# Turned probabilities copied by ScalarE between the two sides' exponentials, masked ones against differences of values

## The chip, the core and the metric

The kernel runs on one core of a Trainium2 chip. The metric is device microseconds of one execution, the median of several. Five engines run side by side, each through its own queue in order: TensorE (PE in the profile, its weight loads PEld), VectorE (DVE), ScalarE (ACT), GpSimd (POOL) and SyncE (SP), which here only issues transfers. An engine waits for another through semaphores.

## The reference

One layer of a decoder over 1024 prompt tokens and 8 x 4 sample tokens, in float32, D = 1024. The part that the change touches is the attention of the prompt over a sliding window of 128 keys, with 8 heads in 2 key-value groups of 4 and a learned sink for each head:

```python
def _sink_attention(q, k, v, mask, sinks):
    s = jnp.einsum('bnqhgd,bnkhd->bnhgqk', q, k).astype(jnp.float32) * (HEAD_DIM ** -0.5)
    s = jnp.where(mask[None, :, None, None], s, -jnp.inf)
    sink = sinks.astype(jnp.float32)[None, None, :, :, None, None]
    m = jnp.maximum(jnp.max(s, axis=-1, keepdims=True), sink)
    p = jnp.exp(s - m)
    denom = jnp.sum(p, axis=-1, keepdims=True) + jnp.exp(sink - m)
    w = (p / denom).astype(v.dtype)
    return jnp.einsum('bnhgqk,bnkhd->bnqhgd', w, v)
```

Each of the 8 blocks of 128 queries looks at its own block's keys up to the query and at the previous block's keys behind it. Around it stand the input projection (q, k, v and a pooling mixer), the output projection with norms, a SwiGLU feed-forward and a gated per-layer input.

## The kernel before

Matrix products are made of three float32r matmuls for each tile (high x high, high x low, low x high); "splits" (L173 on ScalarE, L174 on VectorE) make the high and low parts of weights and activations. The stages are the input projections (to about 128 us), the attention with the first output projections between its blocks (to about 214 us), the rest of the output projection, the feed-forward, and the gated input.

In the attention each block goes through these steps. A "side" is one key-value group, four heads; a key and the one 128 before it share a column, since a query sees just one of the two.

- `scores(b)`: matmuls on TensorE; four copies from PSUM on ScalarE (L775) and four predicated copies on VectorE (L779), which put the current block's score or the previous block's score into one tile `t` of 128 columns a head. For block 0 VectorE adds a mask instead (L781).
- `weigh(t)`: for each of the two sides a `softmax`: the maximum (L721), its negative with scale and sink (`nmx`, L723) and the sink's part (`es`, L725) on VectorE; on ScalarE the exponential of `es` (L729) and four exponentials of a head each, with sums (L732); the sum and reciprocal on VectorE (L737, L738); the scaling by it on GpSimd (L740).
- `turned(b, t)`: four transposes a side on TensorE into one PSUM bank (L122), then two multiplications by a mask on VectorE, from that bank: `ptc` (L800) keeps what belongs to the current block's values, `ptp` (L802) what belongs to the previous block's. Block 0 has no `ptp`.
- `values(b, parts)`: for each half of the queries a matmul a side on `ptc`, then one on `ptp`, summed in PSUM; `put` brings the result to the operands of the output projection (L711 on ScalarE, L712 on VectorE). The values stand in `vtok` by block and in `vmix` with the two blocks' halves mixed.

The blocks go in the order 6, 7, 5, 0, 1, 2, 3, 4. One turn of the loop does: scores and weights of the next block, a filler, `turned` and, after another filler, `values` of this one. A filler is a piece of the output projection: `out_pool` and `out_attn` with 12 matmuls, `out_proj` with 24. Behind `out_attn`, VectorE adds (L912), and ScalarE squares (L899, L902) and scales (L914); behind `out_proj`, ScalarE scales (L922) and squares (L902). Behind `out_pool` ScalarE copies (L893).

On TensorE the order is the written one. On the other engines a scheduler decides it when the program is built, except for instructions that `keep_in_program_order` pins among themselves. In the attention before, only the last turn's VectorE instructions are pinned (through `fix`). Tiles named `a` come from one pool of 30 slots.

Of the kernel before, what the change touches and what calls it, by code (L numbers as in the profile page):

```python
# [12 lines left out]
AF = mybir.ActivationFunctionType  # L13
ALU = mybir.AluOpType
AX = mybir.AxisListType

P = 128
# [3 lines left out]
NDEC, DSEQ = 8, 4  # L21
# [11 lines left out]
NB = SEQ // WIN  # L33
# [12 lines left out]
NEG = -1.0e30  # L46
# [16 lines left out]
def trunk_kernel(  # L63
# [33 lines left out]
    te, ve, se, ge = nc.tensor, nc.vector, nc.scalar, nc.gpsimd  # L97
# [10 lines left out]
    def nm(s):  # L108
        cnt[0] += 1
        return f"{s}{cnt[0]}"  # L110

    def act_tile(shape, dt=F32, s="a"):
        return apool.tile(shape, dt, tag="a", bufs=A_SLOTS, name=nm(s))
# [6 lines left out]
    def mt(out, src):  # L120

        ins = te.transpose(out, src, ident)  # L122
        if pinned[0]:
            tc.keep_in_program_order(ins)

    def mm(*args, **kw):

        ins = te.matmul(*args, **kw)  # L128
        if pinned[0]:
            tc.keep_in_program_order(ins)  # L130

    def bank():
        return psum.tile([P, 512], F32, tag="b", name=nm("b"))
# [33 lines left out]
    def fix(ins):  # L167

        if fixed[0]:
            tc.keep_in_program_order(ins)  # L170
# [493 lines left out]
    nc.scalar.dma_start(ps_o, pso)  # L664


    misc = act_tile([P, 6, P])
    qd, am, vdec = misc[:, 0, :], misc[:, 1:5, :], misc[: NDEC * DSEQ, 5, :]
    for c in range(4):
        ge.tensor_copy(  # L670
            qd.rearrange("p (g c e) -> p g c e", g=4, c=4)[:, :, c, :],
# [6 lines left out]
    ge.tensor_scalar(nskd, skd, -1.0, None, op0=ALU.mult)  # L678


    vtok, vmix = act_tile([P, NB, P]), act_tile([P, NB, P])

    def v_turned():
        for h in range(2):
            ps = bank()
            for i in range(4):
                b = 4 * h + i
                mt(ps[:, i * P : (i + 1) * P], vT[:, b * P : (b + 1) * P])
            v = ps.rearrange("p (b c) -> p b c", c=P)
            se.copy(vtok[:, 4 * h : 4 * h + 4, :], v)  # L690
            ge.tensor_copy(vmix[0:64, 4 * h : 4 * h + 4, :], vtok[0:64, 4 * h : 4 * h + 4, :])
        ge.tensor_copy(vmix[64:P, 1:NB, :], vtok[64:P, 0 : NB - 1, :])
        ps = bank()
        mt(ps[: NDEC * DSEQ, :P], vT[:, SEQ:])
        se.copy(vdec, ps[: NDEC * DSEQ, :P])
        nc.scalar.dma_start(kp_o, kT[:, SEQ - WIN : SEQ])
        nc.scalar.dma_start(vp_o, vtok[:, NB - 1, :])
# [17 lines left out]
    def softmax(*parts):  # L715

        scale = 0.125
        held = []
        for t, nh, sk, nsk in parts:
            mx = spool.tile([P, nh], F32, tag="mx", name=nm("mx"))  # L720
            fix(ve.tensor_reduce(mx, t, axis=AX.X, op=ALU.max))  # L721
            nmx = spool.tile([P, nh], F32, tag="nmx", name=nm("nmx"))
            fix(ve.scalar_tensor_tensor(nmx, mx, -scale, nsk, op0=ALU.mult, op1=ALU.min))  # L723
            es = spool.tile([P, nh], F32, tag="es", name=nm("es"))
            fix(ve.tensor_tensor(es, sk, nmx, op=ALU.add))  # L725
            held.append((nmx, es))
        sums = []
        for (t, nh, _, _), (nmx, es) in zip(parts, held):
            se.activation(es, es, AF.Exp)  # L729
            sm = spool.tile([P, nh], F32, tag="sm", name=nm("sm"))  # L730
            for c in range(nh):
                se.activation(  # L732
                    t[:, c, :], t[:, c, :], AF.Exp, bias=nmx[:, c : c + 1], scale=scale, accum_out=sm[:, c : c + 1]
                )
            sums.append(sm)
        for (t, nh, _, _), (_, es), sm in zip(parts, held, sums):
            fix(ve.tensor_tensor(sm, sm, es, op=ALU.add))  # L737
            fix(ve.reciprocal(sm, sm))  # L738
            nk = t.shape[2]
            ge.tensor_tensor(t, t, sm.unsqueeze(2).to_broadcast([P, nh, nk]), op=ALU.mult)  # L740

    def m4(i):
        return am[:, i, :].unsqueeze(1).to_broadcast([P, 4, WIN])

    def v4(a):
        return a.rearrange("p (c k) -> p c k", k=WIN)

    def scores(b, now_=True):


        t = act_tile([P, 8, WIN])
        nk = 2 * WIN if b else WIN
        lo = b * WIN + WIN - nk
        at = WIN * 4 // nk
        both = [[bank() for _ in range(4 // at)] for _ in range(2)]
        sides = [(0, 64, 64, 0, 192), (64, P, 64, 128, 128), (64, P, 192, 64, 64)] if b else [(0, P, 0, 0, nk)]
        for c in range(4):
            i = c % at
            for q0, q1, at0, k0, n in sides:
                for kv in range(2):  # L760
                    rows = slice(64 * kv, 64 * kv + 64)
                    mm(
                        both[kv][c // at][q0:q1, i * nk + at0 : i * nk + at0 + n],
                        qT[c][rows, b * WIN + q0 : b * WIN + q1],
                        kT[rows, lo + k0 : lo + k0 + n],
                        start=True,
                        stop=True,
                    )
        for kv in range(2):
            tk = t[:, 4 * kv : 4 * kv + 4, :]  # L770
            for i, ps in enumerate(both[kv]):
                tc_ = tk[:, i * at : (i + 1) * at, :]
                v = ps.rearrange("p (c k) -> p c k", k=nk)
                if b:
                    se.copy(tc_, v[:, :, 64:192])  # L775
                    m = am[:, 0, :].rearrange("p (h k) -> p h k", h=2).unsqueeze(1).to_broadcast([P, at, 2, 64])
                    other = v[:, :, 192:].unsqueeze(2).to_broadcast([P, at, 2, 64])
                    tch = tc_.rearrange("p c (h k) -> p c h k", h=2)
                    ve.copy_predicated(tch, m.bitcast(mybir.dt.int32), other)  # L779
                else:  # L780
                    ve.tensor_tensor(tc_, v, m4(1), op=ALU.add)  # L781
        if now_:
            weigh(t)
        return t

    def weigh(t):
        for kv in range(2):
            hs = slice(4 * kv, 4 * kv + 4)
            softmax((t[:, hs, :], 4, skp[:, hs], nskp[:, hs]))

    def turned(b, t):

        ptc = act_tile([P, 8, WIN])
        ptp = act_tile([P, 8, WIN]) if b else None
        for kv in range(2):
            ps = bank()
            hs = slice(4 * kv, 4 * kv + 4)
            for c in range(4):
                mt(ps[:, c * P : (c + 1) * P], t[:, 4 * kv + c, :])
            fix(ve.tensor_tensor(ptc[:, hs, :], v4(ps), m4(2), op=ALU.mult))  # L800
            if b:
                fix(ve.tensor_tensor(ptp[:, hs, :], v4(ps), m4(3), op=ALU.mult))  # L802
        return ptc, ptp

    def values(b, parts):


        ptc, ptp = parts
        sides = [(kv, slice(64 * kv, 64 * kv + 64), slice(4 * kv, 4 * kv + 4)) for kv in range(2)]
        if not b:  # L810
            o = bank()
            for kv, cols, hs in sides:
                mm(o[cols, :], vtok[:, b, cols], ptc[:, hs, :], start=True, stop=True)
            put(o, 0, WIN)
            return
        q = [slice(0, 64), slice(64, P)]
        os_ = [bank() for _ in range(2)]
        for i, v in enumerate((vmix, vtok)):
            for kv, cols, hs in sides:
                mm(os_[i][cols, :256], v[:, b, cols], ptc[:, hs, q[i]], start=True, stop=False)  # L820
        for i in range(2):
            for kv, cols, hs in sides:
                mm(os_[i][cols, :256], vtok[q[i], b - 1, cols], ptp[q[i], hs, q[i]], start=False, stop=True)
        for i in range(2):
            put(os_[i], b * WIN + 64 * i, 64)

# [117 lines left out]
    t = scores(order[0], False)  # L944
# [1 line left out]
    filler(1)  # L946
    od = bank()
    pt = dturned(td)
    weigh(t)
    filler(2)  # L950
    ahead = scores(order[1])
    dvalues(pt, od)
# [7 lines left out]
    for a, b in zip(order, order[1:] + [None]):  # L960

        fixed[0] = lazy[0] = b is None
        t2 = ahead or (None if b is None else scores(b))
        ahead = None
        filler(1)
        parts = turned(a, t)
        if b is None:
            lazy[0] = False
            weights(WOA[1][0], 1)
        filler(1)  # L970
        values(a, parts)
        t = t2
# [192 lines left out]
    os_ = [None] * G  # L1165
# [309 lines left out]
def _layout(i):  # L1475

    f = lambda a: np.asarray(a, dtype=np.float32) if not isinstance(a, np.ndarray) else a
    i = {k: f(v) for k, v in i.items()}
# [7 lines left out]
    gains = np.stack([i[n][0].reshape(KC, P).T for n in ("norm_mix_pre", "norm_mix_post", "norm_ffn_pre", "norm_ffn_post")], 1)  # L1486
    sinks = i["attn_sinks"][0]
    q, c = np.arange(WIN)[:, None], np.arange(WIN)[None, :]
    masks = np.stack([1.0 * np.where(q < 64, c <= q, c > q), np.where(c <= q, 0.0, NEG), 1.0 * ((q <= c) | ((q >= 64) & (c < 64))), 1.0 * (q > c)], 1)
    r = np.arange(P)[:, None]  # L1490
    ri, rj = (r % 8) // DSEQ, r % DSEQ
    rb = 2 * (r // 32) + ri
# [57 lines left out]
```

## Time and profile before

| what | before |
|---|---|
| median of 3 runs | 1076.01 us |
| the runs | 1075.78, 1076.01, 1079.14 us |
| the profiled execution's own time | 1077.23 us |
| its span, first to last instruction | 1075.4 us |
| granted TensorE clock, mean | 0.999 |
| attention stage, 127 to 215 us: VectorE busy | 70.36 us of 88 |
| the same: ScalarE busy | 63.19 us of 88 |

The profile is of one execution. A row of its groups gives the line, the engine, the operation, output and input tiles without their numbers, the shape, the count, the busy time and the mean length, then the idle time of the engine just ahead of it and who ended it. A row of the timeline gives start, length and the same names, with x the number of merged instructions. Starts follow each other more closely than the lengths, since the instructions of an engine overlap a little.

### The profile page before, as it was taken

Reading aid. Unit: us, or ns where it says so; the run is one execution under the profiler, and the core shown is the slowest. Engines: PE = TensorE matmul, PEld = TensorE weight load, DVE = VectorE, ACT = ScalarE, POOL = GpSimd, SP = SyncE. Lnnn points to the kernel's source line nnn. Section 1 sums busy time; section 2 is a strip of 40 time slices with the busy share of each in tenths; the row PEclk is TensorE's granted clock in tenths of the full one; section 3 lists DMA queues with packets and bytes.
Section 4 is the critical chain, followed back from the end, with each engine's and each line's share of the span. In section 5 each row is a group of like instructions: output and inputs, shape, how many; then the busy total and the mean of one; then the engine's idle time right before and its main releaser. Section 6 shows DMA issues by size and latency. Waiting matters only on the chain.

```text
span 1075.4 us, 18180 instructions
## 1 busy us (share of the span) xinstructions
PE 1068.5 (99%) x7107; PEld 1051.6 (98%) x7107; DVE 872.4 (81%) x1303; ACT 512.2 (48%) x872; POOL 275.6 (26%) x211
## 2 busy tenths in 40 slices
PE   9999999999999999999999999999999999999998
PEld 8999988899999999999999999999999999999998
DVE  6876378886979957796698898898899998969983
ACT  7423277664555533445543443443444465545441
POOL 0073032100000024444444454454442000023300
PEclk9999999999999999999999999999999999999999
DMA  8121311544544422422212213212234556464361
GB/s 300 59 73 40 104 58 37 202 157 144 200 165 137 137 99 79 138 74 84 84 70 86 91 60 98 79 60 98 79 114 174 179 170 249 153 212 156 99 211 62
DMA packets 43574, 130.91 MB, mean 122 GB/s; under 512 B 5060, under 2 KB 15716, under 8 KB 43488
## 3 DMA queue, kind: packets, MB, share of 16 engines
q1 hardware_dynamic: 42160, 127.98, 34.9%
q10 hardware_dynamic: 1328, 1.77, 0.5%
q8 instruction: 56, 0.92, 0.3%
q14 instruction: 30, 0.25, 0.1%
HBM read 113.86 MB, written 15.87 MB: 121 GB/s over the span
## 4 chain that ended last, share of the span: by engine, by line
PE 95%; ACT 2%; DVE 2%; DMA 0%; issue 0%; SPq 0%; ACTq 0%; DVEq 0%
PE b L128 95%; ACT a L732 1%; DMA xr<-in_x_dram 0%; DVE mx L721 0%; PE b L122 0%; DVE a L779 0%; DVE wl L174 0%; DVE ml L712 0%; ACT wh L173 0%; DVE sm L737 0%; DVE a L781 0%; ACT y L914 0%; ACT sq L902 0%; ACT y L922 0%; ACT es L729 0%
## 5 line engine op out<-in xcount | busy, mean ns | idle before, releaser
L1108 POOL TENSOR_TENSOR wr<-wr,wr 128x512 f32<-128x512 f32 x108 | 170.0, 1588 | 480.0 <-DMA wr<-in_w_gu_dram 247.9
L173 ACT CAST wh<-wr 128x1024 fp32r<-128x1024 f32 (+1 forms) x138 | 142.0, 1031 | 165.2 <-PE b L128 97.9
L174 DVE TENSOR_TENSOR wl<-wr,wh 128x1024 fp32r<-128x1024 f32 (+1 forms) x138 | 172.7, 1254 | 42.4 <-ACT wh L173 21.2
L128 PE MATMUL b<-fh,wh 128*128 128x352 f32 x624 | 201.5, 323 | 0.0
L128 PE MATMUL b<-fh,wl 128*128 128x352 f32 x624 | 200.0, 320 | 0.0
L128 PE MATMUL b<-fl,wh 128*128 128x352 f32 x624 | 199.9, 320 | 0.0
L128 PE MATMUL b<-fh,sh 128*128 128x352 f32 x416 | 134.3, 323 | 0.0
L128 PE MATMUL b<-fl,sh 128*128 128x352 f32 x416 | 133.3, 320 | 0.0
L128 PE MATMUL b<-fh,sl 128*128 128x352 f32 x416 | 133.3, 320 | 0.0
L173 ACT CAST sh<-wr 128x1024 fp32r<-128x1024 f32 x72 | 75.7, 1052 | 120.1 <-POOL wr L1108 119.7
L174 DVE TENSOR_TENSOR sl<-wr,sh 128x1024 fp32r<-128x1024 f32 x72 | 98.3, 1366 | 36.1 <-ACT sh L173 20.0
L128 PEld LDWEIGHTS b<-fh,wh 128*128 128x128 f32 x624 | 117.0, 187 | 0.4
L128 PEld LDWEIGHTS b<-fl,wh 128*128 128x128 f32 x624 | 117.2, 188 | 0.0
L128 PEld LDWEIGHTS b<-fh,wl 128*128 128x128 f32 x624 | 117.1, 188 | 0.0
L128 PE MATMUL b<-h,wh 128*128 128x352 f32 x480 | 105.3, 324 | 0.6 <-ACT h L449 0.3
L128 PE MATMUL b<-hid,wh 128*128 128x352 f32 x416 | 99.4, 322 | 0.0
L128 PEld LDWEIGHTS b<-h,wh 128*128 128x128 f32 x480 | 81.6, 188 | 2.1 <-DVE h L451 1.2
L128 PEld LDWEIGHTS b<-fl,sh 128*128 128x128 f32 x416 | 78.2, 188 | 0.0
L128 PEld LDWEIGHTS b<-fh,sh 128*128 128x128 f32 x416 | 78.0, 188 | 0.1
L128 PEld LDWEIGHTS b<-fh,sl 128*128 128x128 f32 x416 | 78.0, 188 | 0.0
L1108 POOL TENSOR_TENSOR wr<-wr 128x512 f32<-128x512 f32 x36 | 50.2, 1393 | 108.1 <-DVE w L174 103.6
L128 PE MATMUL b<-hp,sh 128*128 128x352 f32 x320 | 76.4, 322 | 0.0
(202 smaller groups left out, 2217.9 us busy)
## 6 DMA issues: line engine op xcount, KB each, us to landing
wr<-in_w_gu_dram SPq DMA_DIRECT2D x88, 512.0 KB, 3.3
wr<-in_w_dn_dram SPq DMA_DIRECT2D x40, 512.0 KB, 3.3
wr<-in_w_pg_dram SPq DMA_DIRECT2D x16, 512.0 KB, 3.6
x<-in_x_dram SPq DMA_DIRECT2D x6, 704.0 KB, 8.6
x1d<-x SPq DMA_DIRECT2D x6, 704.0 KB, 3.6
x<-x1d SPq DMA_DIRECT2D x6, 704.0 KB, 5.1
out_y_dram<-yo SPq DMA_DIRECT2D x24, 176.0 KB, 2.1
wr<-in_w_out_b_dram SPq DMA_DIRECT2D x8, 512.0 KB, 3.3
```

The source lines that it names most:

```text
L128: ins = te.matmul(*args, **kw)
L173: fix(se.copy(hi, src))
L174: fix(ve.tensor_tensor(lo, src, hi.bitcast(F32), op=ALU.subtract))
L732: se.activation(t[:, c, :], t[:, c, :], AF.Exp, bias=nmx[:, c : c + 1], scale=scale, accum_out=sm[:, c : c + 1])
L1108: ge.tensor_tensor(out, a, b, op=op)
```

## The change

The probabilities for the current block are no longer masked. ScalarE copies them whole from PSUM into `ptc`. What belongs to the previous block is then counted with the current block's values too, and the masked part `ptp` meets the difference of the two blocks' values (`vdif`, made once by GpSimd), which takes the wrong one out and puts the right one in. For block 0 the probabilities above the diagonal are zero already. The number and shapes of matmuls stay as they were.

The order is changed with it. `scores` now weighs only side 0 of the next block; side 1 is weighed after this block's `turned`. All exponentials of heads and the new copies are pinned in the order written, so that the copies stand between the two sides' exponentials on ScalarE.

```diff
-    vtok, vmix = act_tile([P, NB, P]), act_tile([P, NB, P])
+    vtok, vmix, vdif = (act_tile([P, NB, P]) for _ in range(3))
...
         ge.tensor_copy(vmix[64:P, 1:NB, :], vtok[64:P, 0 : NB - 1, :])
+        ge.tensor_tensor(vdif[:, 1:NB, :], vtok[:, 0 : NB - 1, :], vtok[:, 1:NB, :], op=ALU.subtract)
...
             for c in range(nh):
-                se.activation(
-                    t[:, c, :], t[:, c, :], AF.Exp, bias=nmx[:, c : c + 1], scale=scale, accum_out=sm[:, c : c + 1]
+                tc.keep_in_program_order(
+                    se.activation(
+                        t[:, c, :], t[:, c, :], AF.Exp, bias=nmx[:, c : c + 1], scale=scale, accum_out=sm[:, c : c + 1]
+                    )
                 )
...
         if now_:
-            weigh(t)
+            weigh(t, 0)
         return t
 
-    def weigh(t):
-        for kv in range(2):
+    def weigh(t, *sides):
+        for kv in sides:
...
-            fix(ve.tensor_tensor(ptc[:, hs, :], v4(ps), m4(2), op=ALU.mult))
+            tc.keep_in_program_order(se.copy(ptc[:, hs, :], v4(ps)))
             if b:
-                fix(ve.tensor_tensor(ptp[:, hs, :], v4(ps), m4(3), op=ALU.mult))
+                fix(ve.tensor_tensor(ptp[:, hs, :], v4(ps), m4(2), op=ALU.mult))
...
-                mm(os_[i][cols, :256], vtok[q[i], b - 1, cols], ptp[q[i], hs, q[i]], start=False, stop=True)
+                mm(os_[i][cols, :256], vdif[q[i], b, cols], ptp[q[i], hs, q[i]], start=False, stop=True)
...
-    weigh(t)
+    weigh(t, 0, 1)
...
         parts = turned(a, t)
+        if t2:
+            weigh(t2, 1)
```

The table of masks loses the one that `ptc` met, so that `m4(2)` is now what `m4(3)` was.

The order of instructions shows what the scheduler made of it. First, ScalarE in the turn of block 7, where the scores in `a_1650` (before) or `a_1652` (now) are block 5's. Before:

```order
L173 CAST wh_1980<-wr_1949 128x1024
L732 ACTIVATE a_1650,sm_1694<-a_1650,nmx_1689 128x128 x2
L729 ACTIVATE es_1691<-es_1691 128x4
L732 ACTIVATE a_1650,sm_1694<-a_1650,nmx_1689 128x128 x2
L729 ACTIVATE es_1706<-es_1706 128x4
L732 ACTIVATE a_1650,sm_1709<-a_1650,nmx_1704 128x128 x4
L893 COPY y_1286<-b_1717 128x352
L893 COPY y_1287<-b_1747 128x352
```

The same place now; `a_1718` is `ptc` of block 7:

```order
L173 CAST wh_1982<-wr_1936 128x1024
L730 ACTIVATE es_1693<-es_1693 128x4
L734 ACTIVATE a_1652,sm_1696<-a_1652,nmx_1691 128x128 x4
L896 COPY y_1286<-b_1704 128x352
L803 COPY a_1718<-b_1720 128x512
L803 COPY a_1718<-b_1727 128x512
L730 ACTIVATE es_1738<-es_1738 128x4
L734 ACTIVATE a_1652,sm_1741<-a_1652,nmx_1736 128x128 x4
L896 COPY y_1287<-b_1749 128x352
```

The two copies stand behind one side's exponentials and behind the copy of a filler's result, and ahead of the other side's exponentials.

Second, ScalarE in the turn of block 1; the scores are block 2's (`a_2023`, now `a_2025`). Before:

```order
L173 CAST wh_2124<-wr_1984 128x1024
L711 CAST mh_2019<-b_2016 128x4x128
L775 COPY a_2023<-b_2024 128x256
L775 COPY a_2023<-b_2026 128x256
L775 COPY a_2023<-b_2025 128x256
L775 COPY a_2023<-b_2027 128x256
L173 CAST wh_2240<-wr_2128 128x1024
L732 ACTIVATE a_2023,sm_2067<-a_2023,nmx_2062 128x128 x2
L729 ACTIVATE es_2064<-es_2064 128x4
L732 ACTIVATE a_2023,sm_2067<-a_2023,nmx_2062 128x128 x2
L729 ACTIVATE es_2079<-es_2079 128x4
L732 ACTIVATE a_2023,sm_2082<-a_2023,nmx_2077 128x128 x4
```

Now, from the second of the two casts of weights (`wh`) on; the first stands behind the cast of `mh` instead of ahead of it:

```order
L173 CAST wh_2227<-wr_2130 128x1024
L905 ACTIVATE sq_2091<-y_1287 128x352
L917 ACTIVATE y_1287<-y_1287,c_72 128x352
L730 ACTIVATE es_2066<-es_2066 128x4
L734 ACTIVATE a_2025,sm_2069<-a_2025,nmx_2064 128x128 x4
L803 COPY a_2095<-b_2097 128x512
L803 COPY a_2095<-b_2104 128x512
L730 ACTIVATE es_2115<-es_2115 128x4
L734 ACTIVATE a_2025,sm_2118<-a_2025,nmx_2113 128x128 x4
```

The square and the scaling of the `out_attn` result (L902 and L914 before, L905 and L917 now) stood behind all exponentials and now stand ahead of the first side's.

Third, VectorE at the same place. Before:

```order
L174 TENSOR_TENSOR wl_2125<-wr_1984,wh_2124 128x1024
L712 TENSOR_TENSOR ml_2020<-b_2016,mh_2019 128x4x128
L779 COPY_PREDICATED a_2023<-a_1280,b_2024 128x256
L779 COPY_PREDICATED a_2023<-a_1280,b_2026 128x256
L779 COPY_PREDICATED a_2023<-a_1280,b_2025 128x256
L779 COPY_PREDICATED a_2023<-a_1280,b_2027 128x256
L721 TENSOR_REDUCE mx_2060<-a_2023 128x4
L721 TENSOR_REDUCE mx_2075<-a_2023 128x4
L723 SCALAR_TENSOR_TENSOR nmx_2062<-mx_2060,c_1289 128x4
L912 TENSOR_TENSOR y_1287<-y_1287,b_2090 128x352
L725 TENSOR_TENSOR es_2064<-c_75,nmx_2062 128x4
```

Now:

```order
L713 TENSOR_TENSOR ml_2022<-b_2018,mh_2021 128x4x128
L174 TENSOR_TENSOR wl_2127<-wr_1986,wh_2126 128x1024
L782 COPY_PREDICATED a_2025<-a_1280,b_2026 128x256
L782 COPY_PREDICATED a_2025<-a_1280,b_2027 128x256
L782 COPY_PREDICATED a_2025<-a_1280,b_2028 128x256
L782 COPY_PREDICATED a_2025<-a_1280,b_2029 128x256
L722 TENSOR_REDUCE mx_2062<-a_2025 128x4
L915 TENSOR_TENSOR y_1287<-y_1287,b_2077 128x352
L724 SCALAR_TENSOR_TENSOR nmx_2064<-mx_2062,c_1289 128x4
L722 TENSOR_REDUCE mx_2111<-a_2025 128x4
L726 TENSOR_TENSOR es_2066<-c_75,nmx_2064 128x4
```

The addition of the `out_attn` result (L912, now L915) went from behind both sides' maxima to between them, ahead of the first side's `nmx`, and the split of weights (`wl`) from ahead of `ml` to behind it.

More of the change, by code (lines that the diff above doesn't have):

```diff
@@ L664, in trunk_kernel @@
     nc.scalar.dma_start(ps_o, pso)
-    misc = act_tile([P, 6, P])
-    qd, am, vdec = misc[:, 0, :], misc[:, 1:5, :], misc[: NDEC * DSEQ, 5, :]
+    misc = act_tile([P, 5, P])
+    qd, am, vdec = misc[:, 0, :], misc[:, 1:4, :], misc[: NDEC * DSEQ, 4, :]
     for c in range(4):
@@ L1488, in _layout @@
     q, c = np.arange(WIN)[:, None], np.arange(WIN)[None, :]
-    masks = np.stack([1.0 * np.where(q < 64, c <= q, c > q), np.where(c <= q, 0.0, NEG), 1.0 * ((q <= c) | ((q >= 64) & (c < 64))), 1.0 * (q > c)], 1)
+    masks = np.stack([1.0 * np.where(q < 64, c <= q, c > q), np.where(c <= q, 0.0, NEG), 1.0 * (q > c)], 1)
     r = np.arange(P)[:, None]
```

## The prediction

> **What bounds the kernel now.** I read the page first, for the busy shares and the chain that ended last, and then the waits of TensorE, to see what it ever lacks.
>
> ```profile
> span 1075.4 us, 18180 instructions
> PE 1068.5 (99%) x7107; PEld 1051.6 (98%) x7107; DVE 872.4 (81%) x1303; ACT 512.2 (48%) x872; POOL 275.6 (26%) x211
> PE 95%; ACT 2%; DVE 2%; DMA 0%; issue 0%; SPq 0%; ACTq 0%; DVEq 0%
> PE b L431 <- POOL c L156: 1.6, 1, 1.6
> PE b L128 <- DVE a L800: 0.5, 1, 0.5
> ```
>
> TensorE is busy for 99% of the span and carries 95% of the chain; its one listed wait in the attention stage is 0.5 us, for L800, an instruction that the change takes away. The change leaves TensorE's order and its number of matmuls as they are, and no engine's order differs behind the attention stage. So the time can move only by TensorE's stalls between 147 and 214 us. Its timeline shows them.
>
> ```profile
> 146.87 1.04 PE L122 MATMUL b<-c,a 128*128 128x128 f32 x8
> 149.75 3.01 PE L128 MATMUL b<-a,a 128*64 128x256 f32 x64
> 157.60 2.77 PE L128 MATMUL b<-a,a 128*64 128x256 f32 x32
> 165.20 3.66 PE L128 MATMUL b<-a,a 128*64 128x256 f32 x64
> 185.09 3.01 PE L128 MATMUL b<-a,a 128*64 128x256 f32 x64
> 190.07 1.27 PE L122 MATMUL b<-c,a 128*128 128x128 f32 x8
> 195.14 0.65 PE L128 MATMUL b<-a,a 128*64 128x256 f32 x2
> 196.27 3.01 PE L128 MATMUL b<-a,a 128*64 128x256 f32 x62 [0.48 <-DVE a L800]
> 206.03 1.68 PE L128 MATMUL b<-a,a 128*64 128x256 f32 x16
> ```
>
> A turn is named by the block whose probabilities are turned in it: 6, 7, 5, 0, 1, 2, 3, 4. The rows of 149.75, 157.60, 165.20, 185.09, 195.14 and 206.03 are the starts of `values` in turns 6, 7, 5, 1, 2 and 3, with the next scores merged in. Sixty-four matmuls take 3.01 us unhindered; turn 5 takes 3.66, a stall of 0.65. Turn 2 starts two matmuls at 195.14 and the rest at 196.27, 1.13 late, and its transposes take 1.27 instead of 1.04, 0.23 late. **All that could be won is thus 0.65 + 1.13 + 0.23 = 2.0 us**, 0.19% of the span; about 0.3% is what a measurement of this kernel can tell from no change.
>
> **The change, part by part.**
>
> ```profile
> L732 ACT ACTIVATE a<-a,nmx 128x128 f32<-128x128 f32 x56 | 21.7, 389 | 10.1 <-DVE nmx L723 10.1
> L800 DVE TENSOR_TENSOR a<-b,a 128x512 f32<-128x512 f32 x16 | 10.9, 683 | 1.5 <-PE b L122 1.4
> L740 POOL TENSOR_TENSOR a<-a,sm 128x512 f32<-128x512 f32 x14 | 15.9, 1133 | 48.4 <-DVE sm L738 43.5 <-issue 5.0
> 128.56 1.07 ACT L690 COPY a<-b 128x512 f32<-128x512 f32 x2 [7.25 <-PE b L122]
> 134.66 1.15 POOL L740 TENSOR_TENSOR a<-a,sm 128x576 f32<-128x576 f32 x1 [3.31 <-ACT a L775]
> 158.57 1.84 POOL L740 TENSOR_TENSOR a<-a,sm 128x512 f32<-128x512 f32 x1 [6.39 <-DVE sm L738]
> 137.33 0.82 PE L122 MATMUL b<-c,a 128*128 128x128 f32 x6
> ```
>
> VectorE loses the 16 multiplications of L800, 10.9 us of busy time, all beside TensorE's matmuls but for the waits above. ScalarE gains 16 copies of the same shape; two in a row take 1.07 at L690, so one is 0.48 from start to start and 0.58 to its end: 16 x 0.48 = 7.7 us. L802 stays. GpSimd gains one subtraction over 128x896; no row shows it. From below it is nothing; from above 896/512 of the longest L740, 1.84, is 3.2 us. I take 896/512 x 1.04, the length of an undisturbed L740, = 1.8. It stands in the 3.31 us that GpSimd idled ahead of the sample tokens' multiplication (134.66), whose transposes come at 137.33: within 3.3 us it costs nothing, and 1.5 more are free behind it.
>
> What counts is where the copies wait. The products of side 0 and side 1 are what `values` starts on; so far VectorE made them as soon as it was free. Now both copies stand in ScalarE's queue behind side 0's exponentials of the next block, and those behind VectorE's maxima. Queued behind the copies are side 1's exponentials, then the sums on VectorE and the scaling on GpSimd. That tail is not late: exponentials 1.64, sum and reciprocal 0.35, L740 1.04 make 3.0 us, and the next transposes come 4.9 us after `values` starts (3.01 and a filler of 12 matmuls, 1.9).
>
> ```profile
> 149.38 0.93 ACT L893 COPY y<-b 128x352 f32<-128x352 f32 x2
> 154.75 1.05 ACT L173 CAST wh<-wr 128x1024 fp32r<-128x1024 f32 x1 [1.29 <-PE b L128]
> 155.70 0.40 ACT L732 ACTIVATE a<-a,nmx 128x128 f32<-128x128 f32 x1
> 158.99 0.78 ACT L893 COPY y<-b 128x352 f32<-128x352 f32 x2
> 156.77 0.68 DVE L800 TENSOR_TENSOR a<-b,a 128x512 f32<-128x512 f32 x1
> ```
>
> Both sides' exponentials run from 155.70 to 158.99 without a gap, so one side is 1.64 (0.10 for `es`, 4 x 0.385). Two copies end 0.48 + 0.58 = 1.06 after that.
>
> **Turn 6.** The copy of the out_pool result, after the exponentials before (149.38), now stands ahead of them and waits for TensorE's filler, which ends at 146.87 + 0.2: ScalarE is free at 147.41, exponentials to 149.05, copies to 150.11, `values` at 150.17 instead of 149.75: **+0.4**.
>
> **Turn 7.** L173 waits for a buffer that TensorE frees at 154.73, now 0.4 later: 155.17; exponentials from 156.12 to 157.76, one L893 of 0.33 to 158.09, copies to 159.15. `values` would start at 157.60 + 0.4 = 158.0 and starts at 159.2: **+1.2**. Before, L800 was through at 156.77 + 0.68 = 157.45, because it waited for no exponential.
>
> **Turn 5.** The copies stand around side 0's exponentials: side 0's transposes end 0.64 after their start at 162.31 + 1.6 (half of the 1.04 and a hop), copy 0.48, exponentials 1.64, copy 0.58: 167.25. The stall is 0.5 instead of 0.65: **-0.15**. **Turns 0 and 4:** in turn 0 the filler ahead of `values` has 24 matmuls, 3.9 us, and the copies end 0.5 ahead of need; in turn 4 no exponentials are left: **0**.
>
> ```profile
> 176.54 1.04 ACT L173 CAST wh<-wr 128x1024 fp32r<-128x1024 f32 x1
> 174.75 0.48 ACT L899 ACTIVATE acc<-y 128x352 f32<-128x352 f32 x1
> 175.26 0.59 ACT L914 ACTIVATE y<-y,c 128x352 f32<-128x352 f32 x1
> 175.75 0.54 ACT L922 ACTIVATE y<-b,c 128x352 f32<-128x352 f32 x1
> 177.47 0.59 ACT L711 CAST mh<-b 128x512 fp32r<-128x512 f32 x1
> 177.95 1.21 ACT L775 COPY a<-b 128x256 f32<-128x256 f32 x4
> 177.61 1.23 DVE L174 TENSOR_TENSOR wl<-wr,wh 128x1024 fp32r<-128x1024 f32 x1 [0.25 <-ACT wh L173]
> 179.36 1.44 DVE L779 COPY_PREDICATED a<-a,b 128x256 f32<-128x256 int32 x4
> 180.68 1.27 DVE L721 TENSOR_REDUCE mx<-a 128x4 f32<-128x512 f32 x2
> 181.94 0.51 DVE L912 TENSOR_TENSOR y<-y,b 128x352 f32<-128x352 f32 x1
> 187.86 1.30 POOL L740 TENSOR_TENSOR a<-a,sm 128x512 f32<-128x512 f32 x1 [1.82 <-DVE sm L738]
> 188.28 1.95 DVE L174 TENSOR_TENSOR wl<-wr,wh 128x1024 fp32r<-128x1024 f32 x1
> 203.36 0.40 ACT L732 ACTIVATE a<-a,nmx 128x128 f32<-128x128 f32 x1 [1.99 <-DVE nmx L723]
> ```
>
> **Turn 1.** Here ScalarE's order is worse than only two copies longer: the square and the scaling of the out_attn result (L899 or L902, L914), so far behind the exponentials, now stand ahead of them, and the square waits for VectorE's L912. In turn 0 that ends at about 173.0, so the second side's exponentials end at 178.1 (before: 174.75). Then, step by step: L922 0.44, square 0.35, L711 0.48, L173 0.94; on VectorE L174 1.2, L779 1.32, one maximum 0.6, L912 0.43, to 183.95; on ScalarE square 0.52, L914 0.49, exponentials 1.64, copies 1.06: 187.8. `values` was due at 185.09 + 1.45 = 186.55: **+1.25**.
>
> **Turn 2.** Side 1's exponentials to 189.3, L922 and square 0.79, two casts 0.54, L173 0.94, L174 1.2, L779 1.32, maximum 0.6, L912 0.43, square and scaling 1.0, exponentials 1.64, copies 1.06: `values` at 199.05, 2.8 behind the old 196.27. The old stalls of 1.13 and 0.23 go and as much comes: **+0.05**. I take L174 at 1.23, though it took 1.95 at 188.28 beside L740 (187.86 to 189.16), since L740 now ends before it starts; were they still side by side, 0.7 more.
>
> The Trainium skill, "SBUF — State Buffer", has a rule on this pair: VectorE with two SBUF inputs and GpSimd share one port pair as an exclusive lock, and the later one waits the other out (section "Who interferes with whom"). The rows agree: 189.16 + 1.2 is 190.4, against 190.23. By it the sum stands as long as L740 is through; a 1.04 us L740 just ahead would make turn 2 cost up to 1.04 more.
>
> **Turn 3.** `values` was due at 206.03 + 2.8 = 208.85; exponentials that began at 203.36 now begin behind a square at about 205.8, and with L914 between them and the copies these end at 209.0: **+0.2**.
>
> Sum: 0.4 + 1.2 - 0.15 + 1.25 + 0.05 + 0.2 = **+3.0 us** (2.95). The span would be 1078.4 and that execution's own time 1077.2 + 3.0 = 1080.2; the median of the runs shown, 1076.0, lies 1.2 under the profiled time, so I forecast 1079.0. L802's successor waits for its copy and ends 0.7 after it; `values` needs it 1.0 after its own start, so it costs nothing.
>
> **The rivals.** (a) *The relief wins.* VectorE, free of 0.6 us a side, brings the maxima earlier, and the copies come in time. For it: ScalarE idles 10.1 us ahead of L732, all for `nmx`. Against: the maxima wait for score copies and L912, not for L800. At best all stalls go: -2.0, 1074.0. (b) *Slower beyond the bound: ScalarE and VectorE become a ring longer than TensorE's turn.* The place is turns 1 and 2, where I reckon 11.3 us from copies to copies against 9.9 us on TensorE. Each 0.1 us more in the ring is paid in both, and in turns 6, 7 and 3 with its copies. It decides from a sum of 3.2, that is from 0.05 us more in each of five turns; with 0.2 to 0.8 more in each (0.7 is L174 beside L740) it is 4 to 7 us: 1080 to 1083. (c) *TensorE's clock falls in the longer gaps.* The longest gap so far in this stage, 1.13 us, left the granted clock at 1.00:
>
> ```profile
> 127.00:215.00 88.00, 87.46 (x915) 76.52 (x915) 70.36 (x182) 63.19 (x234) 22.29 (x22) 1.00 0.29 97
> ```
>
> Three gaps of 1.2 to 1.4 us are little longer. If each halved the clock over the next 3.0 us of matmuls, that would add 1.5 each: 3.0 + 4.5, 1083.5. The Trainium skill, "TensorE: Matmul & The Clock Gate", Part 1 on the gate, lets an idle window of some 3.4 us halve the clock; by that rule gaps of 1.4 us leave it alone, and the trace agrees as far as 1.13 us. (d) *The change does not do what it says*: the order shows the copies between the two sides in seven turns of eight, so no chance of its own.
>
> **How the numbers follow.** The forecast, +1.8 to +4.2 (each of five late turns off by up to 0.25), has 0.62; (a) 0.20, from -2.0 to +1.8; (b) 0.15; (c) 0.03. Slower by over 0.3% (above 1079.2) are some 0.26 of the forecast's 0.62, all of (b) and (c): 0.44. Faster by over 0.3% (below 1072.8) needs more than all stalls: 0.03, for what I have overlooked. Within: 0.53. The range 1075.6 to 1081.6 leaves out the lower half of (a), the upper half of (b), and (c).
>
> **What would show it.** TensorE's waits would name the new copies (the line of `se.copy(ptc...)`) in turns 7, 1 and 2 with about 1 us each, in 6, 5 and 3 with less; the starts of `values` would drift to 3.0 us behind the old ones by turn 3 and stay there; VectorE would be some 11 us less busy, ScalarE 8 us more. Wrong would be: `values` on time in turn 7 (then the queue is not strict as I read it), stalls at the transposes (then side 1's tail is late), or a granted clock under 1.00.

## The result and the profile after

| | before | after | ratio (95%) |
|---|---|---|---|
| time, median | 1076.68 us (1075.78 to 1079.14, 6 runs) | 1082.13 us (1081.37 to 1084.58, 6 runs) | 1.0054 (1.0041 to 1.0066) |
| profiled execution, own time | 1077.23 | 1081.37 | |

The change costs 5.45 us by the medians. The forecast was 3.0 us, 1079.0, with a range up to 1081.6: the sign was right, the size too small, and the time lies where rival (b) put it (1080 to 1083, chance 0.15).

The page of the changed kernel, its span and its busy shares:

```profile
span 1079.6 us, 18177 instructions
PE 1068.6 (99%) x7107; PEld 1051.3 (97%) x7107; DVE 859.1 (80%) x1287; ACT 518.7 (48%) x888; POOL 275.9 (26%) x212
```

VectorE is 13.3 us less busy (872.4 before) and ScalarE 6.5 us more (512.2), close to the 11 and 8 forecast. TensorE works as long as before, for the same 7107 matmuls. What is new is its waits; first the list of them, then the window of the attention stage (the last figures are granted clock, DMA share and GB/s):

```profile
PE b L128 <- ACT a L803: 4.2, 4, 1.5
PE b L431 <- POOL c L156: 1.6, 1, 1.6
```

```profile
127.00:215.00 88.00, 83.78 (x877) 73.11 (x876) 60.09 (x161) 65.42 (x242) 23.10 (x23) 1.00 0.27 89
```

Before, 0.5 us of waits stood here, for VectorE's L800. Now TensorE waits four times for L803, ScalarE's new copy, and it is busy for 83.8 of 88 us instead of 87.5. The clock stays at 1.00. TensorE's timeline shows where; the rows are the starts of `values` in turns 6, 7, 5, 1, 2 and 3:

```profile
149.88 3.42 PE L128 MATMUL b<-a,a 128*64 128x256 f32 x64
158.86 3.24 PE L128 MATMUL b<-a,a 128*64 128x256 f32 x32 [0.65 <-ACT a L803]
166.94 3.50 PE L128 MATMUL b<-a,a 128*64 128x256 f32 x64
188.10 3.49 PE L128 MATMUL b<-a,a 128*64 128x256 f32 x64 [1.51 <-ACT a L803]
199.67 3.49 PE L128 MATMUL b<-a,a 128*64 128x256 f32 x64 [1.25 <-ACT a L803]
210.79 2.15 PE L128 MATMUL b<-a,a 128*64 128x256 f32 x16 [0.81 <-ACT a L803]
```

The waits in brackets are 0.65 (turn 7), 1.51 (turn 1), 1.25 (turn 2) and 0.81 (turn 3), together 4.2. Where 64 matmuls take 3.49 instead of 3.01, the first product was there and the second not yet: the second copy ends 0.48 behind the first.

Since TensorE's order is the same in all kernels, each matmul's start can be set against the same matmul's start before. How much this difference grows in a turn is what the turn costs (us; the first column is the forecast, the others are of the profiled executions, with the offset at 145 us, up to 0.94, taken away):

| turn | forecast | change | e1 | e4 | e9 | e2 | e10 |
|---|---|---|---|---|---|---|---|
| 6 | +0.4 | +0.41 | 0.00 | +0.41 | 0.00 | 0.00 | 0.00 |
| 7 | +1.2 | +1.19 | +1.19 | +1.19 | 0.00 | 0.00 | 0.00 |
| 5 | -0.15 | -0.17 | +0.02 | -0.17 | +1.21 | +0.24 | +0.42 |
| 0 | 0 | -0.13 | -0.13 | -0.13 | -0.13 | -0.13 | -0.16 |
| 1 | +1.25 | **+2.03** | +0.50 | +1.91 | +0.54 | 0.00 | 0.00 |
| 2 | +0.05 | **+0.42** | +0.12 | +0.18 | +0.10 | -1.16 | -1.40 |
| 3 | +0.2 | **+1.35** | +0.22 | +0.40 | +0.22 | +2.27 | +0.17 |
| 4 | 0 | 0.00 | 0.00 | -0.01 | 0.00 | +0.76 | +0.02 |
| sum | +2.95 | +5.10 | +1.92 | +3.78 | +1.94 | +1.96 | -0.95 |

So the miss has a place. Turns 6, 7, 5 and 0 came out as reckoned; turns 1, 2 and 3 cost 3.80 instead of 1.50. Behind the stage most of the profiled executions win back 0.5 to 1.4 us on that of before (e3 0.7, although it has the order of before there); that is a difference between executions, not of the change.

### The profile page after: what moved, and what is told of

It is laid out like the page before. It is cut to its first block, busy times and chain, and to the rows that moved or that the text cites. A ratio compares the mean times of both kernels' runs of the same rounds, so it can differ in the third digit from the quotient of the medians.

```text
span 1079.6 us, 18177 instructions
## 1 busy us (share of the span) xinstructions
PE 1068.6 (99%) x7107; PEld 1051.3 (97%) x7107; DVE 859.1 (80%) x1287; ACT 518.7 (48%) x888; POOL 275.9 (26%) x212
## 4 chain that ended last, share of the span: by engine, by line
PE 92%; ACT 3%; DVE 3%; DMA 1%; issue 1%; SPq 0%; ACTq 0%; DVEq 0%
PE b L128 92%; ACT a L734 2%; DMA xr<-in_x_dram 1%; DVE a L782 1%; ACT a L803 0%; DVE mx L722 0%; SPq L425 0%; DVE ml L713 0%; PE b L122 0%; ACT xr L459 0%; DVE wl L174 0%; ACT sq L905 0%; DVE h L451 0%; ACT h L449 0%; ACT wh L173 0%
## 5 line engine op out<-in xcount | busy, mean ns | idle before, releaser
L174 DVE TENSOR_TENSOR wl<-wr,wh 128x1024 fp32r<-128x1024 f32 (+1 forms) x138 | 169.8, 1234 | 44.9 <-ACT wh L173 23.7
L174 DVE TENSOR_TENSOR sl<-wr,sh 128x1024 fp32r<-128x1024 f32 x72 | 95.4, 1326 | 35.6 <-ACT sh L173 18.9
```

Of the source, the lines that this page charges most:

```text
L174: fix(ve.tensor_tensor(lo, src, hi.bitcast(F32), op=ALU.subtract))
```

## The experiments

Theory A: the copies are late by what stands ahead of them in ScalarE's queue, in turns 1 to 3 the square and the scaling of the `out_attn` result. Theory B: VectorE sets the ring, since its addition of squares waits for GpSimd's scaling of the probabilities.

A row of an experiment has the line numbers of its own file: the exponentials (L734 after) are L743 or L744 there, the copies (L803) L801, L804, L812 or L813, and likewise the rest.

**e3: the new masking alone.** VectorE copies, in the order of before.

```diff
-            fix(ve.tensor_tensor(ptc[:, hs, :], v4(ps), m4(2), op=ALU.mult))
+            fix(ve.tensor_copy(ptc[:, hs, :], v4(ps)))
...
+        ge.tensor_tensor(vdif[:, 1:NB, :], vtok[:, 0 : NB - 1, :], vtok[:, 1:NB, :], op=ALU.subtract)
```

> The kernel before with the new masking alone: VectorE copies the turned probabilities in place of the multiplication by the mask, GpSimd makes the difference of the values, both sides are weighed before, nothing is pinned. If the cost of the change lies in ScalarE's queue (A) or in the ring of VectorE and GpSimd (B): within 0.5 us of before, 1076.7. If the difference of the values or the copy itself costs (the rest of the change): up to the change's own +5 us.

Measured: 1076.70 against 1076.73, ratio 0.9998 (0.9989 to 1.0007); no turn moves by more than 0.03 us. The masking, the difference of the values and GpSimd's subtraction cost nothing. So the 5 us come from the copies being on ScalarE and from the order.

**e8: the copies alone.** As e3, with nothing pinned, but:

```diff
-            fix(ve.tensor_copy(ptc[:, hs, :], v4(ps)))
+            se.copy(ptc[:, hs, :], v4(ps))
```

> The new masking with ScalarE's copies, but nothing else of the change: both sides are weighed before, nothing is pinned, and the scheduler puts the copies in turns 6 and 7 behind both sides' exponentials and in turns 1 to 3 the second one behind the square as well. If the copies are late by what stands ahead of them on ScalarE: 1.0 in turn 6, some 1 to 1.8 in turn 7, 1.2 to 1.5 in each of turns 1 to 3, together 6 us over before: 1081 to 1084. If it is the change's order (its pins, the two sides apart) that costs, and not the copies on ScalarE: within 1 us of before, 1077.

Measured: 1087.16, ratio 1.0091 (1.0076 to 1.0107), 10.4 us over before. The copies' late place costs as A says, and more than reckoned: from turn 6 to turn 3 the turns cost 1.06, 4.39, 1.49, 0.92, 1.54, 0.51 and 0.75 us. Turn 7 is far over, turns 5 and 0, for which nothing was reckoned, add 2.4, and turns 2 and 3 stay under. In turn 7, TensorE's timeline and the windows of one microsecond (granted clock third from the right) of e8:

```profile
160.75 4.80 PE L128 MATMUL b<-a,a 128*64 128x256 f32 x32 [2.28 <-ACT a L801]
```

```profile
161.00:162.00 1.00, 1.00 (x7) 0.55 (x6) 1.00 (x2) 0.52 (x2) 0.54 (x1) 0.86 0.00 0
162.00:163.00 1.00, 1.00 (x6) 0.31 (x8) 0.02 (x1) 0.00 (x0) 0.00 (x0) 0.50 0.00 0
163.00:164.00 1.00, 1.00 (x10) 0.25 (x4) 0.00 (x0) 0.12 (x1) 0.00 (x0) 0.50 0.00 0
164.00:165.00 1.00, 1.00 (x12) 1.00 (x14) 0.72 (x2) 0.53 (x2) 0.00 (x0) 0.50 0.00 0
165.00:166.00 1.00, 1.00 (x11) 0.88 (x10) 0.46 (x2) 0.00 (x0) 0.00 (x0) 0.94 0.00 0
```

Behind a wait of 2.28 us the clock is halved for some 3.4 us. What is lost is 0.14 + 3 x 0.50 + 0.06 = 1.7 us, on top of the wait. So rival (c) exists, but in the profiled execution of the change, with gaps of up to 1.51, the clock stayed at 1.00. Against the place that the scheduler gives such copies unpinned, the change's order saves 5 us, 1.7 of it the clock's; e1 shows an order that is better still.

**e1: the square and the scaling behind the exponentials.**

```diff
-            tc.keep_in_program_order(se.copy(ptc[:, hs, :], v4(ps)))
+            behind(lambda: se.copy(ptc[:, hs, :], v4(ps)))
...
-        squares_into(acc[g], yv, m == 0)
-        se.activation(yv, yv, AF.Identity, scale=gn[:, 1, m : m + 1])
+        if defer[0]:
+            late.append((m, g, yv))
...
             weigh(t2, 1)
+        tails()
```

`behind` queues each exponential and each copy behind the one of these written before it, and nothing else; `tails` issues the square and the scaling there.

> The change as it is, but in turns 0 to 3 the square and the scaling of the out_attn result stand on ScalarE behind the exponentials of both sides, as before the change; the copies stay between the sides. Theory A (the copies are late by what stands ahead of them in ScalarE's queue, and in turns 1 to 3 that is the square and the scaling, which wait for VectorE's addition): the copies of turns 1 to 3 end 1.2 to 1.3 us earlier against the exponentials' maxima, turn 1 costs 0.8 instead of 2.1, the sum goes from +5.2 in this stage to +3.5, and the time is 1.6 us under the change's: about 1080.5. Theory B (the ring is set by VectorE, whose addition of squares waits for GpSimd's scaling of the probabilities): the square and the scaling only move behind the exponentials, the next turn still begins behind them, no more than 0.5 us is won: 1081.6 or more.

Measured: 1078.58, ratio 1.0021 (1.0012 to 1.0030): 3.5 us under the change, twice what A forecast, and far from B's 0.5. Turns 1 to 3 cost 0.84 instead of 3.80, and turn 6 nothing instead of 0.41. ScalarE in turn 1, of the change and then of e1:

```profile
184.83 0.50 ACT L905 ACTIVATE sq<-y 128x352 f32<-128x352 f32 x1 [1.94 <-DVE y L915]
...
185.85 0.19 ACT L730 ACTIVATE es<-es 128x4 f32<-128x4 f32 x1
187.49 1.04 ACT L803 COPY a<-b 128x512 f32<-128x512 f32 x2
```

```profile
183.93 0.40 ACT L743 ACTIVATE a<-a,nmx 128x128 f32<-128x128 f32 x1 [1.51 <-DVE nmx L733]
185.58 1.04 ACT L812 COPY a<-b 128x512 f32<-128x512 f32 x2
188.17 0.49 ACT L914 ACTIVATE sq<-y 128x352 f32<-128x352 f32 x1
```

In the change, the exponentials begin at 185.85, 1.02 behind a square that has itself waited 1.94 for the addition. In e1 they begin at 183.93, released by their own maxima, and the copies start 1.9 us earlier (185.58 against 187.49); 0.4 of that is only that e1's turn 1 began earlier (its transposes at 181.32 against 181.71).

**e4: the addition of squares taken off VectorE.** In `out_proj` of the change, and nothing else:

```diff
-        squares_into(acc[g], ps[:, : NS[g]], False)
+        squares_into(acc[g], ps[:, : NS[g]], False, eng=ge)
```

> The change as it is, but the squares of out_proj's results are added by GpSimd and not by VectorE, so that no addition stands ahead of the split and the maxima on VectorE and waits out GpSimd's scaling. Theory B: the ring is shorter by 0.4 us in turn 1, 0.4 in turn 2 and 0.8 in turn 3, 1.6 in all: 1080.5. Theory A: the wait is covered by the cast of the weights, which ends as late: 0.4 us or less, 1081.7.

Measured: 1080.31, ratio 1.0042 (1.0029 to 1.0054): 1.8 us under the change by the medians, nearer to B's number than to A's; the two intervals overlap, so the turns have to decide. In the stage e4 wins 1.32 us: 0.12 in turn 1, 0.24 in turn 2 and 0.95 in turn 3, where B had 0.4, 0.4 and 0.8. Both theories hold, since they speak of two links of one ring. The link that B names, in the change: VectorE from the end of turn 0 to `nmx` of turn 1, and the same addition in the next two turns; then GpSimd's scaling beside each.

```profile
179.48 1.23 DVE L906 TENSOR_TENSOR acc<-acc,sq 128x352 f32<-128x352 f32 x1 [0.34 <-ACT sq L905]
180.64 0.68 DVE L713 TENSOR_TENSOR ml<-b,mh 128x512 fp32r<-128x512 f32 x1
181.24 1.21 DVE L174 TENSOR_TENSOR wl<-wr,wh 128x1024 fp32r<-128x1024 f32 x1
182.37 1.43 DVE L782 COPY_PREDICATED a<-a,b 128x256 f32<-128x256 int32 x4
183.69 0.67 DVE L722 TENSOR_REDUCE mx<-a 128x4 f32<-128x512 f32 x1
184.29 0.50 DVE L915 TENSOR_TENSOR y<-y,b 128x352 f32<-128x352 f32 x1
...
191.00 1.22 DVE L906 TENSOR_TENSOR acc<-acc,sq 128x352 f32<-128x352 f32 x1 [0.34 <-ACT sq L905]
...
202.56 1.22 DVE L906 TENSOR_TENSOR acc<-acc,sq 128x352 f32<-128x352 f32 x1 [0.34 <-ACT sq L905]
```

```profile
179.29 1.04 POOL L743 TENSOR_TENSOR a<-a,sm 128x512 f32<-128x512 f32 x1 [2.01 <-DVE sm L741]
...
190.80 1.04 POOL L743 TENSOR_TENSOR a<-a,sm 128x512 f32<-128x512 f32 x1 [1.53 <-DVE sm L741]
...
202.36 1.04 POOL L743 TENSOR_TENSOR a<-a,sm 128x512 f32<-128x512 f32 x1 [1.53 <-DVE sm L741]
```

In each turn the addition starts 0.2 us behind L743 and ends 0.4 us after it: it takes 1.22 us. Where nothing of GpSimd stands beside it, in e1's turn 1, the same addition takes 0.53 (the row of GpSimd there ends at 178.73):

```profile
178.75 0.53 DVE L915 TENSOR_TENSOR acc<-acc,sq 128x352 f32<-128x352 f32 x1 [1.21 <-ACT sq L914]
```

```profile
177.69 1.04 POOL L752 TENSOR_TENSOR a<-a,sm 128x512 f32<-128x512 f32 x1 [1.52 <-DVE sm L750]
```

That e4 wins so little in turn 1 has the same reason. GpSimd makes the addition there, behind L743, and now the split of weights (L174) starts beside it and takes 1.42 us instead of 1.21. GpSimd and VectorE in turn 1 of e4:

```profile
180.09 0.96 POOL L906 TENSOR_TENSOR acc<-acc,sq 128x352 f32<-128x352 f32 x1
```

```profile
180.72 1.42 DVE L174 TENSOR_TENSOR wl<-wr,wh 128x1024 fp32r<-128x1024 f32 x1 [0.27 <-ACT wh L173]
```

**e5: e1 and e4 together.**

> e1 and e4 together: the square and the scaling behind both sides' exponentials, and out_proj's squares added by GpSimd. If both take links out of one ring, which counts only as far as it is longer than TensorE's turn, the gains don't add: e1 left 0.5, 0.1 and 0.2 us in turns 1 to 3, so at most 0.8 us more than e1: 1077.8 (1077.4 to 1078.6). If they are separate costs, they add, 3.5 and 1.8 us under the change: 1076.8 or less.

Measured: 1079.45, ratio 1.0022 (1.0014 to 1.0031); in this stage 1.92, as e1 alone. The gains don't add. What is left of turns 1 to 3 is the same 0.84 us in both. In the median e5 is even 0.9 us over e1, which the stage doesn't show. In the one profiled execution of each, e5 was 0.94 us behind before when it came to 145 us, and e1 0.03 ahead; whether that is so in the other runs is open.

**e6: each copy twice.**

```diff
-            tc.keep_in_program_order(se.copy(ptc[:, hs, :], v4(ps)))
+            for _ in range(2):
+                tc.keep_in_program_order(se.copy(ptc[:, hs, :], v4(ps)))
```

> The change as it is, but ScalarE makes each copy twice, one behind the other, to the same tile: 0.96 us more in a turn. If the copies stand in a ring of ScalarE and VectorE that is longer than TensorE's turn in turns 1 to 3, and behind side 0's exponentials in turns 6, 7 and 5, each of these six turns pays 0.96 and turn 0 hands 0.96 on to turn 1: 5.5 to 6.7 us over the change, 1087.6 to 1088.8. If what costs is the order and not the time on ScalarE, since ScalarE is busy for 48% only: up to 1 us over the change, 1083.

Measured: 1098.57, ratio 1.0198 (1.0184 to 1.0212), 16.4 us over the change, more than either expectation. Two sizes were off. A copy to the tile that the copy ahead has just written waits for that one's end; ScalarE in turn 6 of e6:

```profile
149.81 0.57 ACT L804 COPY a<-b 128x512 f32<-128x512 f32 x1
150.76 1.05 ACT L804 COPY a<-b 128x512 f32<-128x512 f32 x2
152.10 0.58 ACT L804 COPY a<-b 128x512 f32<-128x512 f32 x1
```

The four take 2.87 us from 149.81 to 152.68; the two of the change take 1.04, so 1.83 were added to a turn and not 0.96. And three gaps (turns 7, 1 and 3) halved the clock, at 1.7 us each by the windows. In the profiled execution the stage costs 20.40, 15.3 more than the change; less 5.1 for the clock that is 10.2, 5.6 times 1.83. With the clock taken off, each of the seven turns with exponentials to make pays between 0.9 and 1.85 us, as the ring has it, although ScalarE is busy for half of the span.

**e9: in turns 6 and 7 the copies ahead of both sides' exponentials.** As e1, with the scores of these turns not weighed in `scores`, and:

```diff
-            weigh(t2, 1)
+            weigh(t2, *((0, 1) if a in (6, 7) else (1,)))
```

> e1, but in turns 6 and 7 both copies stand ahead of both sides' exponentials. Turn 6 costs nothing in e1 already; turn 7 costs 1.2 of e1's 1.8 us, since its copies stand behind side 0's exponentials, which begin only behind a cast of weights. If that is the cause, values of turn 7 is on time and 1.2 us are won: 1077.4. If side 1's exponentials, now 0.96 later, delay what follows in turn 5 by as much: 0.5 us or less, 1078.1 to 1078.6.

Measured: 1078.56, ratio 1.0020 (1.0011 to 1.0029): as e1. Turn 7 is on time, and turn 5 pays 1.21 us, where 0.5 at most was expected. TensorE in turns 7 and 5 of e9:

```profile
158.37 2.77 PE L128 MATMUL b<-a,a 128*64 128x256 f32 x32
167.36 3.49 PE L128 MATMUL b<-a,a 128*64 128x256 f32 x64 [1.32 <-ACT a L812]
```

The stall was not removed but handed on: in turn 5 the copies still stand behind side 0's exponentials, and those wait for `nmx`.

**e2: the copies first in all turns.** As e1, and:

```diff
-            weigh(t, 0)
+            pass
...
-            weigh(t2, 1)
+            weigh(t2, 0, 1)
```

> As e1, but both copies stand ahead of both sides' exponentials, so that they wait for nothing but the transposes. Theory A: values is on time in turns 6, 7 and 1, and the stalls that the kernel before has in turns 5 (0.65) and 2 (1.13) go as well: 1.8 us under before, 1074.9. Theory B: the second side's exponentials end 1 us later, VectorE's addition of squares and the maxima with them, and the stalls move to the transposes: at before's time or up to 2 us over it, 1076.7 to 1079.

Measured: 1079.12, ratio 1.0025 (1.0015 to 1.0035). Both theories had a part: `values` is on time in turns 6, 7 and 1, and turn 2's old stall of 1.13 is gone; then turn 3 loses 2.27 at its transposes. VectorE and ScalarE in turn 2 of e2, ScalarE at the same place before, and TensorE's new wait:

```profile
194.37 1.28 DVE L814 TENSOR_TENSOR a<-b,a 128x512 f32<-128x512 f32 x2
195.57 1.27 DVE L731 TENSOR_REDUCE mx<-a 128x4 f32<-128x512 f32 x2
```

```profile
197.03 0.40 ACT L743 ACTIVATE a<-a,nmx 128x128 f32<-128x128 f32 x1 [3.42 <-DVE nmx L733]
```

```profile
193.60 0.41 ACT L732 ACTIVATE a<-a,nmx 128x128 f32<-128x128 f32 x1 [3.70 <-DVE nmx L723]
```

```profile
PE b L122 <- ACT sq L914: 1.5, 1, 1.5
```

The multiplications by the mask (L814) now stand ahead of the maxima, and the exponentials begin at 197.03 instead of 193.60 before; 0.5 of that is the later start of e2's turn 2 (its transposes at 190.56 against 190.07). The wait is put down to the square, which stands behind these exponentials.

**e7 and e10: a shorter way to the maxima.** As e2, with the addition of the `out_attn` result and the masks queued on VectorE behind `es` of both sides; e7 also has e4's edit.

```diff
-                fix(ve.tensor_tensor(ptp[:, hs, :], v4(ps), m4(2), op=ALU.mult))
+                masked.append((ptp[:, hs, :], v4(ps)))
...
-        ve.tensor_tensor(yv, yv, ps[:, : NS[g]], op=ALU.add)
...
+            with tc.issue_after(vmark[0].ins):
+                ve.tensor_tensor(yv, yv, ps[:, : NS[g]], op=ALU.add)
```

`vmark[0]` is the last `es` on VectorE; the masks are issued behind it in the same way.

> e2 with a shorter way on VectorE: the addition of the out_attn result and the multiplications by the mask stand behind both sides' maxima and not ahead of them, and out_proj's squares are added by GpSimd. e2 lost 1.7 us and more at the transposes of turn 3, since its exponentials of turn 2 began at 197.0 instead of 193.6, behind these instructions. If the ring is what counts, the exponentials of turn 2 begin by 193.5, the transposes of turn 3 are on time, and the stalls of before in turns 5 and 2 are gone: 1.8 us under before, 1074.9. If the copies' own 0.96 us ahead of the exponentials is enough to make side 1's tail late: at the transposes 0.5 to 1 us in turns 0, 2 and 3, so 1076 to 1078.

> e7, but out_proj's squares are added by VectorE again. If e7's gain over e2 (3.4 us) comes from what stands ahead of the maxima (the addition of the out_attn result and the masks): as e7 within 0.5 us, 1075.7 to 1076.2. If VectorE's addition, which waits for GpSimd's scaling, is again what sets the maxima: 0.4 us in each of turns 2 and 3 and in turn 4's start, 1 us or more over e7, 1076.7 to 1077.5.

Measured: e7 1075.72, ratio 0.9990 (0.9981 to 0.9999); e10 1075.46, ratio 0.9991 (0.9983 to 1.0000). They lie 1.1 and 1.2 us under before, 6.4 and 6.7 under the change; against before that is at the edge of what the runs can tell. VectorE and ScalarE in turn 2 of e10, and TensorE's longest wait, but for the 1.6 us for L156 that before and after have too:

```profile
192.37 1.27 DVE L731 TENSOR_REDUCE mx<-a 128x4 f32<-128x512 f32 x2
194.39 1.28 DVE L823 TENSOR_TENSOR a<-b,a 128x512 f32<-128x512 f32 x2
```

```profile
193.95 0.21 ACT L740 ACTIVATE es<-es 128x4 f32<-128x4 f32 x1 [2.10 <-DVE es L735]
```

```profile
PE b L128 <- ACT mh L712: 0.6, 1, 0.6
```

The exponentials begin 3.1 us earlier than in e2, of which 0.4 is the earlier start of the turn (its transposes at 190.14 against 190.56), and no wait for a copy is left. Turn 2 wins 1.40; 0.42 is lost in turn 5, where the cast of the attention result (L712) now stands behind later exponentials. With and without e4's edit it is the same, so here the order of VectorE decides and not GpSimd.

## Why the prediction was wrong

- **What bounds the kernel: right.** TensorE's order and work did not change, and all of the loss is its waits for the new copies.
- **The masking and GpSimd's subtraction: right.** It took 2.11 us (1.8 reckoned, 3.2 as the bound) in the 3.3 that were free; e3 shows no cost.
- **Turns 6, 7, 5: right** to 0.02 us. In turn 7 the copies are behind side 0's exponentials, and those behind the cast of weights; e9 shows it by moving the copies.
- **Turn 0: right for itself** (-0.13 for 0), but what it hands to turn 1 was short: the second side's exponentials end at 178.57 and not at 178.1. The addition of the `out_attn` result, taken to end at 173.0, ends at 173.34, and the square starts 0.12 behind it.
- **Turns 1 and 2: the mechanism right, the size wrong.** The terms listed for turn 1 add to 187.57 and not to 187.8: 0.23 for the way between engines is in the sum without a row. The step that failed is "L174 1.2" right behind its cast, "since L740 now ends before it starts". L174 does take 1.2 us now. But the split L713 has moved ahead of it, as the order showed and the sum left out, and the addition of squares (L906), ahead of both, is what meets GpSimd now: 1.22 us instead of 0.53. L174 starts at 181.24, 0.37 behind the end of its cast (179.81 + 1.06). The same was paid again in turn 2. Of turn 1's miss of 0.78, 0.46 comes from turn 0 and the rest from here. e4, without that addition on VectorE, wins 0.24 of turn 2's miss of 0.37; in turn 1 the wait only moves to L174.
- **Turn 3: the largest miss, 1.15 of 2.15, and the addition left out.** "Exponentials ... now begin behind a square at about 205.8" was not walked through VectorE as turns 1 and 2 were. The ring's links between one turn's exponentials and the next, with VectorE's addition of squares among them, stand nowhere in that term. ScalarE and VectorE before, and the square in the trace after:

```profile
196.89 0.48 ACT L902 ACTIVATE sq<-y 128x352 f32<-128x352 f32 x1
203.16 0.51 DVE L912 TENSOR_TENSOR y<-y,b 128x352 f32<-128x352 f32 x1
```

```profile
207.65 0.50 ACT L905 ACTIVATE sq<-y 128x352 f32<-128x352 f32 x1 [2.49 <-DVE y L915]
```

Before, 6.7 us lie between the end of a turn's exponentials (196.89) and the end of the next addition (203.16 + 0.43). Without the square and the scaling, which stood behind the exponentials there (1.0), these are 5.7. From the reckoned end at 200.7 they lead to 206.4, and with the square to 206.9: 1.1 later than forecast. After, the exponentials end at 201.65 and the square at 208.06, 6.4 us apart. What most of this hangs on, e4 shows: without the addition of squares on VectorE, which takes 1.22 us beside L743 here too, turn 3 costs 0.40 instead of 1.35.
- **The rivals.** (b) was named with its place, and its condition (a ring longer than TensorE's turn) was the forecast's own number, 11.3 against 9.9. It deserved more than 0.15: three of the forecast's own terms hung on that ring. From copies to copies the change takes 11.51, 11.57 and 11.11 us (the starts at 175.98, 187.49, 199.06 and 210.17); e1 takes 11.20, 11.26 and 9.99. (a) was not to be had in this order, where the copies wait for exponentials and not for VectorE's products. (c) stayed away with gaps up to 1.51. The 1.13 us that the prediction took for a gap was a delay; by the same row TensorE's idle time was 0.48, so the trace before vouched for less than it said.
- **The rule on the shared port.** By the Trainium skill, "SBUF — State Buffer" ("Who interferes with whom"), the later of VectorE with two SBUF inputs and GpSimd waits the other out. The trace agrees: L906 took 1.22 us three times, begun 0.2 us behind L743, and L174 took 1.42 in e4, begun 0.6 us behind GpSimd's addition. The prediction applied it to the pair that had shown it before, and not to the instruction that stood there after the change.
- **What set the order: not shown.** In turns 0 to 3 the first copy always stands behind the scaling of the `out_attn` result, which is the ScalarE instruction written just before it. That fits a `keep_in_program_order` which pins an instruction behind the one written just before it on its engine, and so ties the copies to an addition on VectorE. In turns 6 and 7 the filler's copy (L896) stands there, but so it does in e1 without that pin (147.35 and 157.32). e1 both ties the copies to the exponentials alone and moves the square and the scaling behind them; it is 3.5 us faster, and no run separates the two.

The median missed by 3.1 us and the stage by 2.15. The other microsecond lies between executions: the forecast took 1.2 off, by which the profiled one of before was over the median of three runs; over that of six it is 0.55, and the profiled one of after is 0.76 under its median.

## What to carry to other kernels

Where an instruction is moved to a queue behind a wait, walk the whole ring that closes over it, turn by turn, with the new order of every engine in it; a delay that a turn with slack absorbs is still handed on. Taking work off an engine brings nothing unless that engine is on the way: here VectorE was 13 us less busy and the kernel slower, while the place of a square and a scaling in ScalarE's queue was worth 3.5 us. Where an instruction is pinned, look at the built order for what else now stands ahead of it, and pin to the instruction that is meant.

## What the runs showed of the hardware

TensorE in turns 7 and 2 of e6:

```profile
162.27 0.65 PE L128 MATMUL b<-a,a 128*64 128x256 f32 x2 [1.62 <-ACT a L804]
163.62 4.32 PE L128 MATMUL b<-a,a 128*64 128x256 f32 x30 [0.70 <-ACT a L804]
...
211.66 0.65 PE L128 MATMUL b<-a,a 128*64 128x256 f32 x2 [1.77 <-ACT a L804]
213.00 3.01 PE L128 MATMUL b<-a,a 128*64 128x256 f32 x62 [0.70 <-ACT a L804]
```

The first pair of gaps leaves 30 matmuls 4.32 us long, the second leaves 62 at the usual 3.01. TensorE's granted clock was halved behind a wait of 2.28 us in e8, and in e6 behind 1.62 with 0.70 shortly after. The Trainium skill ("TensorE: Matmul & The Clock Gate", Part 1) gives an idle window of some 3.4 us for that; here shorter gaps were enough, and the measurement decides. The clock stayed at 1.00 behind 1.51 in the change and behind the second pair here, so length alone does not decide. Each halving that a trace shows cost 1.7 us. Two of the six runs of the change, 1084.35 and 1084.58, have a mean clock of 0.998 and 0.997 where the others have 0.999 and 1.000; no trace of these runs shows whether a gap was caught there.
